# A one-core hybrid block: the gathered tile of the second layer is routed on its own, ahead of the three dense tiles

## The chip, the cores and the metric

The kernel runs as one program on one core of a Trainium2 chip. The metric is device time in microseconds (us) of one execution. The kernel before was timed three times: 4815.14, 4817.73 and 4818.47 us, median 4817.73 us.

Five engines have instruction streams of their own, each executed in order: PE (TensorE, matmuls; its weight loads are listed as PEld), DVE (VectorE), ACT (ScalarE), POOL (GpSimd) and SP (SyncE, which only issues DMAs here). They meet through semaphores.

## The reference

Two layers on 512 latent tokens (four tiles of 128) and 256 context tokens. Layer 0 mixes tokens with a gated delta rule, layer 1 with windowed attention. Each layer ends with a channel mixer that retrieves experts (PEER), cut here to its core:

```python
def peer_ffn(h, w_query, sub_keys, expert_u, expert_v):
    q = (t @ w_query).reshape(t_count, PEER_HEADS, 2, PEER_HALF)   # 8 heads, two halves of 128
    s = jnp.einsum('thpd,hpkd->thpk', q, sub_keys)                 # 128 keys for each half
    s1, i1 = lax.top_k(s[:, :, 0], 16)
    s2, i2 = lax.top_k(s[:, :, 1], 16)
    cand_s = s1[..., :, None] + s2[..., None, :]                   # 16 x 16 pairs
    top_s, pos = lax.top_k(cand_s, 16)                             # 16 experts for each head
    idx, gate = ..., softmax(top_s)                                # 128 experts for each token
    act = gelu(einsum('pkd,pd->pk', expert_u[idx], h)) * gate
    return einsum('pk,pkd->pd', act, expert_v[idx])
```

In layer 1 it runs for the four latent tiles; a last RMSNorm gives the output.

## The kernel before

**Two ways through the experts.** `peer` (L1327) treats the four tiles in two ways. Three of them are dense tiles: `dense` (L1245) multiplies them by all 16384 experts, 128 blocks of 128, and the chosen experts' gates lie in a mostly empty array G that `gates_dram` (L1204) builds and writes to DRAM. The fourth is the gathered tile: `gather_u` (L1139) and `gather_v` (L1175) fetch, for each of 128 slots, one row of `expert_u` (then of `expert_v`) for each token, with an indirect DMA that POOL issues (L1162, L1189). DVE multiplies a fetched u row tile by the token (`u`, L1164) and sums; PE multiplies v rows by the weights (`po`, L1196; 32 steps of 8 matmuls). Rows land in a ring of UV = 6 buffers.

**The stages of the mixer in layer 1**, as they follow each other:

1. Norm: `peer_norm` (L905) for each tile: mean square on ACT, scaling `xs` on DVE, transposes `pk` on PE, `hk`, and the split of the result into a high and a low half (`hi`, `lo`), so that three fp32r matmuls give one product of nearly full precision (`mm3`, L81).
2. Routing: `peer_route` (L942) goes through 16 queries (8 heads, two halves). For each one it loads 512 KB of weights, splits them (`wh` on ACT, L286; `wl`, L287, on DVE here), does 24 matmuls `pq` over all tiles at once, then scores `pss` for each tile, and for each tile DVE finds the top 16 of 128 with five instructions (L992 to L996, called a set below). After queries 7 and 15, `pairs_of` (L1052) picks 16 pairs for four heads of one tile (a call below: 54 instructions, nearly all on DVE). For the gathered tile the pairs are picked later, inside `gather_u`.
3. Gates: `gates_dram` for each dense tile, one-hot rows on DVE, POOL and ACT, and one matmul `pg` for each token (fp32, which the trace lists as two rows).
4. Dense: for each block of experts `up` does 24 matmuls `pu` (384 columns); for each half of eight blocks `pv` does 144 matmuls (512 columns). Up to 17 results of `up` may wait (RUN = 17), so the scheduler puts 20 `up` blocks (480 matmuls) ahead of the last gate matmul.
5. `finish` (L1115) adds the mixer's output to each tile, and `final` (L1308) norms the four tiles, which it reads back from DRAM.

**What sets the order.** A scheduler orders each engine's stream when the program is built. The gather is a generator: `tick` (L149) lets it go on by some steps at each `up` (from block 16 on) and each `pv` weight load, 1.1 steps each in layer 1. A step is one row fetched. `tick` takes the kinds in turn that `mix` names; for gates, mix "V" asks for v rows alone. Instructions of the gather are pinned to program order. In `peer` of before:

```python
cand = self.peer_route(l, dtiles + gtiles, h + [hk], hdram, p, "left", ps, "u", 3, tg, RAW, c1, nd)
...
for t, (xd, r, gate) in enumerate(gtiles):
    works.extend(self.gather_tile(l, xd, hdram[nd + t], cand[nd + t], gate, gp, rps))
```

So all four tiles share one routing pass, and the gather exists only from the dense stage on.

Of the kernel before, what the change touches and what calls it, by code (L numbers as in the profile page):

```python
# [8 lines left out]
F32 = mybir.dt.float32  # L9
# [9 lines left out]
D = 1024  # L19
# [16 lines left out]
ND = (3, 3)  # L36
UV = 6
EARLY = 6
NORM = 6
ADAF = 7  # L40
RUN = 17
PLAIN = {"out": (0, 1), "route": {"c": 1, "a": 0, "b": 0}}
HG = 4
# [4 lines left out]
CUT = 20  # L48
LATE = (9, 9)
POB = 1  # L50
# [5 lines left out]
LO = 16  # L56
TICK = {"norm": 0, "proj": 0, "z": (0, 0), "mat": (0, 0), "inv": (4, 4), "scan": (2, 4), "out": 2, "swa": 6, "route": 0, "gates": 1,
        ("u", 0): 1.6, ("v", 0): 1.6, ("u", 1): 1.1, ("v", 1): 1.1}

# [7 lines left out]
class Kern:  # L67
    def __init__(self, tc, A, out, dbg=None):
        self.tc, self.nc, self.A, self.out, self.dbg = tc, tc.nc, A, out, dbg or {}
        self.queue = self.nc.sync  # L70
        self.back = []
        self.turn = self.due = 0

    def dma(self, out, in_):
# [867 lines left out]
    def peer_route(self, l, tiles, h, hdram, p, side, ps, pt, bufs, tg, raw, pools, early=6):  # L942
# [74 lines left out]
    def scratch_uv(self, p):  # L1017

        t = lambda shape, dt: p.tile([128] + list(shape), dt, name="pairw", tag="uv", bufs=UV)
        ge, pd, sm = t((8, TOPK, TOPK), BF), t((8, TOPK, TOPK), BF), t((D,), F32)  # L1020
# [118 lines left out]
    def gather_u(self, l, hd, sel, p, ps, this):  # L1139
# [20 lines left out]
        for s in range(SLOTS):  # L1160
            u = p.tile([128, D], F32, name="u", tag="uv", bufs=UV)
            nc.gpsimd.indirect_dma_start(out=u, out_offset=None, in_=A["p_u"],  # L1162
# [12 lines left out]
    def gather_v(self, xd, gate, p, ps, made, j0, j1):  # L1175
# [4 lines left out]
        for j in range(j0, j1):  # L1180
# [5 lines left out]
            for g in range(4):  # L1186
                v = p.tile([128, D], F32, name="v", tag="uv", bufs=UV)
                t = 32 * g + j
# [9 lines left out]
            yield 1  # L1198
        acc = p.tile([128, D], F32, name="gacc", tag="uv", bufs=UV)
        for hf in range(2):  # L1200
            pin(nc.scalar.copy(acc[:, hf * 512:(hf + 1) * 512], po[hf]))
        self.finish(xd, acc, gate, p, UV, nc.gpsimd)

    def gates_dram(self, G, t, ids, gt, p, ps):  # L1204

# [39 lines left out]
    def dense(self, l, tiles, h, G, p, q, gp, ps, works):  # L1245
# [80 lines left out]

    def peer(self, l, gtiles, dtiles, gp, rps, tg):  # L1327

        nd, ng = len(dtiles), len(gtiles)
        with ExitStack() as ctx:  # L1330
            p = ctx.enter_context(self.pool("pp" + tg))
            ps = ctx.enter_context(self.pool("pps" + tg, space=PSUM))
            h = [p.tile([128, KT, 512], F32R, name=n) for n in ("hi", "lo")]
            hdram = [None] * nd + [self.dp.tile([128, D], F32, name=f"h{tg}{t}") for t in range(ng)]
            G = self.dp.tile([32, 128, nd * 4, 4, 32], F32, name=f"G{l}")
            with ExitStack() as c1:
                with ExitStack() as c2:
                    hk = None
                    if PLAIN["route"][tg]:
                        hk = c2.enter_context(self.pool("ph" + tg, "right")).tile([128, KT, 128 * (nd + ng)], F32, name="hk")  # L1340
                    cand = self.peer_route(l, dtiles + gtiles, h + [hk], hdram, p, "left", ps, "u", 3, tg, RAW, c1, nd)
                q = c1.enter_context(self.pool("pb" + tg))
                for t in range(nd):
                    if t == LATE[l]:
                        cand[nd:] = [self.pairs(*c) for c in cand[nd:]]
                    self.gates_dram(G, t, *cand[t], q, ps)
                if LATE[l] == nd:
                    cand[nd:] = [self.pairs(*c) for c in cand[nd:]]
            with ExitStack() as c1:
                q = c1.enter_context(self.pool("pd" + tg))  # L1350
                works = []
                for t, (xd, r, gate) in enumerate(gtiles):
                    works.extend(self.gather_tile(l, xd, hdram[nd + t], cand[nd + t], gate, gp, rps))
                at = len(self.back) - (l == 0 and CUT > 0 and len(self.back) > 1)
                self.back[at:at] = works
# [189 lines left out]
```

## Time and profile before

| | |
|---|---|
| median of three runs | 4817.73 us |
| profiled execution, its time | 4825.25 us |
| its span (first to last instruction) | 4823.5 us |
| granted TensorE clock, mean | 0.935 |
| PE busy | 4180.6 us (87%) |
| DVE busy | 3134.1 us (65%) |
| ACT busy | 1966.9 us (41%) |
| POOL busy | 1559.0 us (32%) |

The busy time is the union of an engine's instructions. A PE that is busy all the time is not yet a PE at its best rate, since ends of matmuls are modelled and overlap; how far apart consecutive matmuls start says more. Layer 1's mixer takes the last third of the span, from 3311 us on.

### The profile page before, as it was taken

The page shows a single profiled execution, that of the slowest core. Times are in us where ns is not written, and L with a number is a line of the kernel's source. Part 1 is how long each engine was busy: PE and PEld are TensorE (multiplying, and loading weights), DVE is VectorE, ACT ScalarE, POOL GpSimd, SP SyncE. Part 2 cuts the span into 40 slices and gives each one's busy share as a digit, 9 for nine tenths or more (in the row PEclk, how much of TensorE's full clock was granted, in tenths as well). Part 3 has the DMA queues.
Part 4 walks back from the last instruction along what each step waited for, and adds up shares of the span by engine and source line. Part 5 has one row for each costly group of instructions (what it writes and reads, how often), then busy time and mean ns, then how long its engine had stood idle before and what let it go on. Part 6 is the DMA issues. An engine that isn't in the chain of part 4 may idle for free. (4 is left out here: it accounts for less than half of the span.)

```text
span 4823.5 us, 66222 instructions
## 1 busy us (share of the span) xinstructions
PE 4180.6 (87%) x23628; PEld 3439.8 (71%) x23628; DVE 3134.1 (65%) x7357; ACT 1966.9 (41%) x3632; POOL 1559.0 (32%) x1393
## 2 busy tenths in 40 slices
PE   7989998457787779999999947797987999999997
PEld 5867777346566569888887725565875898988886
DVE  4664569975798688666764324565986987744444
ACT  5755553322326843333332212443378433333332
POOL 0000022753466652444543332000155343222221
PEclk9989999778899989999999978898999999999999
DMA  6725644978876797899988876102245898766775
GB/s 245 232 94 188 227 143 148 328 261 309 310 267 231 228 339 256 330 340 336 354 318 311 289 248 206 62 18 78 89 127 141 289 346 296 282 243 251 248 260 208
DMA packets 412922, 1142.76 MB, mean 237 GB/s; under 512 B 36656, under 2 KB 152240, under 8 KB 412592
## 3 DMA queue, kind: packets, MB, share of 16 engines
q1 hardware_dynamic: 254352, 563.84, 33.6%
q0 software_dynamic: 158240, 574.69, 33.1%
q8 instruction: 186, 3.05, 0.3%
q14 instruction: 144, 1.18, 0.1%
HBM read 1050.83 MB, written 87.56 MB: 236 GB/s over the span
## 5 line engine op out<-in xcount | busy, mean ns | idle before, releaser
L286 ACT CAST wh<-w 128x1024 fp32r<-128x1024 f32 x636 | 663.7, 1048 | 1248.9 <-PE pu L84 567.6
L287 DVE TENSOR_TENSOR wl<-w,wh 128x1024 fp32r<-128x1024 f32 x604 | 736.0, 1223 | 508.9 <-ACT wh L286 493.1
L1162 POOL DMA_INDIRECT u<-p_u,idx x512 | 641.8, 1254 | 780.7 <-DVE u L1164 418.2
L1189 POOL DMA_INDIRECT v<-p_v,idxT x512 | 532.3, 1040 | 1005.8 <-PE po L1196 681.5
L83 PE MATMUL pu<-lo,wh 128*128 128x384 f32 x2048 | 698.0, 341 | 52.2 <-ACT a L1263 42.4
L1164 DVE SCALAR_TENSOR_TENSOR u<-u,hg 128x1024 f32<-128x1024 f32 x512 | 621.2, 1224 | 185.9 <-DMA u<-p_u,idx 181.5
L85 PE MATMUL pu<-hi,wl 128*128 128x384 f32 x2048 | 697.1, 341 | 10.0 <-POOL wl L287 8.2
L84 PE MATMUL pu<-hi,wh 128*128 128x384 f32 x2048 | 694.6, 339 | 0.0
L83 PE MATMUL pv<-wl,ah 128*128 128x512 f32 x1536 | 600.8, 393 | 2.7 <-DVE acc L1302 2.7
L84 PE MATMUL pv<-wh,ah 128*128 128x512 f32 x1536 | 602.6, 392 | 0.0
L85 PE MATMUL pv<-wh,al 128*128 128x512 f32 x1536 | 602.4, 392 | 0.0
L83 PEld LDWEIGHTS pu<-lo,wh 128*128 128x128 f32 x2048 | 390.0, 190 | 82.1 <-ACT a L1263 54.5
L85 PEld LDWEIGHTS pu<-hi,wl 128*128 128x128 f32 x2048 | 390.0, 190 | 36.7 <-issue 14.9
L84 PEld LDWEIGHTS pu<-hi,wh 128*128 128x128 f32 x2048 | 390.0, 190 | 9.7 <-issue 3.4
L83 PEld LDWEIGHTS pv<-wl,ah 128*128 128x128 f32 x1536 | 289.0, 188 | 81.0 <-issue 12.6
L1196 PE MATMUL po<-v,W 128*32 128x512 f32 x2048 | 267.9, 642 | 90.8 <-DMA v<-p_v,idxT 89.4
L85 PEld LDWEIGHTS pv<-wh,al 128*128 128x128 f32 x1536 | 288.8, 188 | 66.4 <-issue 7.5
L84 PEld LDWEIGHTS pv<-wh,ah 128*128 128x128 f32 x1536 | 288.9, 188 | 58.3 <-issue 4.2
L1239 PE MATMUL pg<-oa,ob 128*128 128x128 f32 x1536 | 267.1, 313 | 72.5 <-POOL ob L1235 47.7
L1239 PEld LDWEIGHTS pg<-oa,ob 128*128 128x128 f32 x1536 | 215.8, 203 | 129.7 <-POOL ob L1235 70.1
L95 ACT CAST ah<-a 128x384 fp32r<-128x384 f32 x256 | 130.9, 514 | 434.2 <-PE pv L84 395.3
L1238 ACT ACTIVATE ob<-hot,gT 128x128 f32<-128x128 bf16 x576 | 253.0, 529 | 18.2 <-DVE hot L1227 15.7
(488 smaller groups left out, 7405.3 us busy)
## 6 DMA issues: line engine op xcount, KB each, us to landing
w<-p_ut SPq DMA_DIRECT2D x256, 512.0 KB, 5.3
w<-p_vt SPq DMA_DIRECT2D x256, 512.0 KB, 5.1
w<-adaw SPq DMA_DIRECT2D x96, 512.0 KB, 5.4
G<-st SPq DMA_DIRECT2D x24, 2048.0 KB, 9.1
Gt<-G SPq DMA_DIRECT2D x64, 768.0 KB, 7.0
w<-g_qkv SPq DMA_DIRECT2D x48, 512.0 KB, 4.8
w<-p_wq SPq DMA_DIRECT2D x32, 512.0 KB, 4.8
w<-g_z SPq DMA_DIRECT2D x16, 512.0 KB, 4.1
```

What stands on the lines that cost most here:

```text
L83: mm(out, lh, rl, start=start, stop=False)
L84: mm(out, lh, rh, start=False, stop=False)
L85: mm(out, ll, rh, start=False, stop=stop)
L95: self.nc.scalar.copy(hi, x)
L286: nc.scalar.copy(hi, w)
L287: (sub or nc.vector).tensor_sub(lo, w, hi)
L1162: nc.gpsimd.indirect_dma_start(out=u, out_offset=None, in_=A["p_u"], in_offset=bass.IndirectOffsetOnAxis(ap=idx[:, s:s + 1], axis=0))
L1164: pin(nc.vector.scalar_tensor_tensor(u, u, 1.0, h, op0=OP.mult, op1=OP.mult, accum_out=w[:, s:s + 1]))
L1189: nc.gpsimd.indirect_dma_start(out=v, out_offset=None, in_=A["p_v"], in_offset=bass.IndirectOffsetOnAxis(ap=idxT[:, t:t + 1], axis=0))
L1196: pin(nc.tensor.matmul(po[hf][32 * g:32 * g + 32, :], W[:, g, :], vs[g][:, hf * 512:(hf + 1) * 512], start=j == j0, stop=j == j1 - 1, tile ...
L1238: nc.scalar.mul(ob[:, j, :], hot[:, :, b % 2 * 4 + j], gT[:, c0 + j:c0 + j + 1])
L1239: nc.tensor.matmul(pg[:, j, :], ob[:, j, :], oa[:, j, :], start=True, stop=True)
```

## The change

The second layer's `peer` is called with `first=True`. Then the gathered tile is normed and routed by a pass of its own (tag "bf", 128 columns, its own weight loads and splits, its pairs picked in the pass), its gather is put into the list of works at once, and the three dense tiles are routed after that, with `tick` letting two rows go on at each query. The first layer's call keeps its order.

```diff
-UV = 6
+RING = (6, 7)
-LATE = (9, 9)
-TICK = {... "route": 0, "gates": 1,
-        ("u", 0): 1.6, ("v", 0): 1.6, ("u", 1): 1.1, ("v", 1): 1.1}
+TICK = {... "route": {"c": 0, "a": 0, "bf": 0, "b": 2}, "gates": (1, 2),
+        ("u", 0): 1.6, ("v", 0): 1.6, ("u", 1): 0.9, ("v", 1): 0.9}
...
-            self.tick(TICK["route"], MIX["route"])
+            self.tick(TICK["route"][tg], MIX["route"])
...
-                    self.tick(TICK["gates"], MIX["gates"])
+                    self.tick(TICK["gates"][l], MIX["gates"])
...
-    def peer(self, l, gtiles, dtiles, gp, rps, tg):
+    def peer(self, l, gtiles, dtiles, gp, rps, tg, first=False):
...
-            h = [p.tile([128, KT, 512], F32R, name=n) for n in ("hi", "lo")]
+            T = 128 * (nd if first else nd + ng)
+            h = [p.tile([128, KT, T], F32R, name=n) for n in ("hi", "lo")]
...
+            if first:
+                with ExitStack() as c1:
+                    q = c1.enter_context(self.pool("pf" + tg))
+                    f = [q.tile([128, KT, 128 * ng], F32R, name=n) for n in ("fhi", "flo")]
+                    cand = self.peer_route(l, gtiles, f + [None], hg, p, "left", ps, "u", 3, tg + "f", RAW, c1, ng)
+                gathered(cand)
+                self.back.extend(works)
             with ExitStack() as c1:
+                tiles, hd = (dtiles, [None] * nd) if first else (dtiles + gtiles, [None] * nd + hg)
...
-                    cand = self.peer_route(l, dtiles + gtiles, h + [hk], hdram, p, "left", ps, "u", 3, tg, RAW, c1, nd)
+                    cand = self.peer_route(l, tiles, h + [hk], hd, p, "left", ps, "u", 3, tg, RAW, c1, nd)
...
-                self.peer(1, tl[:4 - ND[1]], tl[4 - ND[1]:], gp, rps, "b")
+                self.ring = RING[1]
+                self.ip = c1.enter_context(self.pool("ids1"))
+                self.peer(1, tl[:4 - ND[1]], tl[4 - ND[1]:], gp, rps, "b", True)
```

The streams of all engines are the same up to the norm of layer 1's mixer. Three places show what moves.

DVE, from the last instructions of attention's output (`x<-x,y`, L748) on; `nss` and `xs` are the norm, `wl` a weight split, `top` and `ti` the top 16. Before:

```order
L748 TENSOR_TENSOR x<-x,y 128x256
L914 RECIPROCAL nss<-nss 128x1
L915 TENSOR_SCALAR xs<-xs,nss 128x1024
L914 RECIPROCAL nss<-nss 128x1
L915 TENSOR_SCALAR xs<-xs,nss 128x1024
L287 TENSOR_TENSOR wl<-w,wh 128x1024
L926 TENSOR_SCALAR hk<-pk,col_77 128x128
L287 TENSOR_TENSOR wl<-w,wh 128x1024
```

DVE at the same place after the change:

```order
L748 TENSOR_TENSOR x<-x,y 128x256
L914 RECIPROCAL nss<-nss 128x1
L915 TENSOR_SCALAR xs<-xs,nss 128x1024
L287 TENSOR_TENSOR wl<-w,wh 128x1024 x2
L926 TENSOR_SCALAR hk<-pk,col_77 128x128 x4
L932 TENSOR_TENSOR flo<-hk,fhi 128x1024
L287 TENSOR_TENSOR wl<-w,wh 128x1024 x2
L992 MAX top_27926<-sc 128x8
L993 MAX_INDEX ti_27927<-top_27926,sc 128x8
```

The pass of the one tile stands where the norm of the four stood, behind the last instruction of attention; so it does on PE and on ACT. The norm of the dense tiles now stands behind the whole pass, its pairs included.

POOL, from the load of the gathered tile's tokens (`hg`, L1148) to the tile's end; `ob` belongs to the gates, `u` and `v` are the fetched rows. Before:

```order
L1148 DMA hg<-hb_27863 128x1024
L287 TENSOR_TENSOR wl<-w,wh 128x1024 x16
L1235 TENSOR_SCALAR ob<-hot,gT 128x128 x96
L1162 DMA u<-p_u,idx 128x1024 x128
L1189 DMA v<-p_v,idxT 128x1024 x128
```

POOL after the change:

```order
L1148 DMA hg<-hb_27866 128x1024
L1162 DMA u<-p_u,idx 128x1024 x39
L287 TENSOR_TENSOR wl<-w,wh 128x1024 x16
L1235 TENSOR_SCALAR ob<-hot,gT 128x128 x96
L1162 DMA u<-p_u,idx 128x1024 x89
L1189 DMA v<-p_v,idxT 128x1024 x128
```

39 of the 128 u fetches moved ahead of the first dense weight splits and the gates; none stands among the gates. On DVE 32 of the 128 products `u` stand ahead of the gates, 4 in the norm of the dense tiles and 28 in their routing, two in each query.

SP, the last DMAs: `x_105` is the gathered tile in DRAM, `x_106` to `x_108` the dense tiles; `x<-` is a load of `final`, `out<-y` a store of it. Before:

```order
L75 DMA x<-x_105 128x1024
L75 DMA w<-p_vt 128x1024
L75 DMA out<-y 128x1024
L1124 DMA x_106<-xf 128x1024
L1124 DMA x_107<-xf 128x1024
L75 DMA x<-x_106 128x1024
L1124 DMA x_108<-xf 128x1024
L75 DMA x<-x_107 128x1024
L75 DMA out<-y 128x1024
L75 DMA x<-x_108 128x1024
```

SP after the change:

```order
L1124 DMA x_106<-xf 128x1024
L1124 DMA x_107<-xf 128x1024
L1124 DMA x_108<-xf 128x1024
L75 DMA x<-x_105 128x1024
L75 DMA x<-x_106 128x1024
L75 DMA out<-y 128x1024
L75 DMA x<-x_107 128x1024
L75 DMA out<-y 128x1024
L75 DMA x<-x_108 128x1024
```

The gathered tile's load in `final` moved from ahead of the last dense weights to behind the last stores of the dense tiles, and the other loads stand behind it. On PE the last two of the gather's 32 steps (16 matmuls `po`) stand behind the last `pv`; before, the last step stood 162 `pv` ahead of it.

## Rows read from the trace of the kernel before

**Rows 1.** Windows, layer 1's mixer by stage: length, busy (instructions), clock, DMA, GB/s
```profile
core 0: us, PE busy (x) PEld busy (x) DVE busy (x) ACT busy (x) POOL busy (x), PEclk, DMA share, GB/s
3311.00:3342.00 31.00, 10.60 (x41) 7.80 (x41) 15.85 (x30) 19.76 (x37) 0.00 (x0) 0.52 0.48 170
3342.00:3451.00 109.00, 108.34 (x534) 92.10 (x535) 93.13 (x535) 33.16 (x50) 5.32 (x3) 0.98 0.28 93
3451.00:3541.00 90.00, 73.75 (x359) 70.43 (x359) 89.55 (x371) 35.46 (x56) 39.01 (x16) 0.87 0.27 88
3541.00:3728.00 187.00, 158.14 (x880) 125.80 (x878) 142.72 (x207) 176.77 (x359) 106.21 (x94) 0.97 0.49 141
3728.00:3744.00 16.00, 0.00 (x0) 0.00 (x0) 3.22 (x7) 2.63 (x5) 0.00 (x0) 0.52 0.87 280
3744.00:4798.00 1054.00, 1049.75 (x5410) 898.48 (x5410) 641.38 (x966) 354.17 (x486) 296.80 (x259) 1.00 0.75 271
4798.00:4823.50 25.50, 0.00 (x0) 0.00 (x0) 11.40 (x13) 4.33 (x9) 0.00 (x0) 0.55 0.50 185
```

**Rows 2.** Timeline, PE in one query: start, us, engine, line, out<-in, shape, count
```profile
3367.69 1.06 PE L986 MATMUL pss<-sk,qT 128*128 128x128 f32 x8
...
3369.05 0.39 PE L85 MATMUL pq<-hi,wl 128*128 128x512 f32 x1
...
3374.04 1.06 PE L986 MATMUL pss<-sk,qT 128*128 128x128 f32 x8
```

**Rows 3.** Timeline, PE, dense: a run of 46 matmuls of 384 columns
```profile
3842.36 0.33 PE L85 MATMUL pu<-hi,wl 128*128 128x384 f32 x1
...
3850.36 0.39 PE L83 MATMUL pv<-wl,ah 128*128 128x512 f32 x1
```

**Rows 4.** Timeline, PE: attention's projection, matmuls of 256 columns
```profile
2961.47 0.28 PE L85 MATMUL pj<-wh,lo 128*128 128x256 f32 x1
2961.59 0.28 PE L83 MATMUL pj<-wl,hi 128*128 128x256 f32 x1
```

**Rows 5.** Groups of PE by line, dense stage: busy us, mean ns, idle before
```profile
L84 PE MATMUL pv<-wh,ah 128*128 128x512 f32 x768 | 301.3, 392 | 0.0
L84 PE MATMUL pu<-hi,wh 128*128 128x384 f32 x864 | 290.8, 337 | 0.0
L1196 PE MATMUL po<-v,W 128*32 128x512 f32 x512 | 62.6, 598 | 0.0
```

**Rows 6.** Timeline around attention's end and the norm of the four tiles
```profile
3310.54 0.32 SPq L75 DMA_DIRECT2D x<-x  x1
...
3319.06 0.75 DVE L915 TENSOR_SCALAR xs<-xs,nss 128x1024 f32<-128x1024 f32 x1
...
3327.76 1.22 DVE L932 TENSOR_TENSOR lo<-hk,hi 128x1024 fp32r<-128x1024 f32 x1 [0.52 <-ACT hi L931]
...
3340.67 1.22 DVE L932 TENSOR_TENSOR lo<-hk,hi 128x1024 fp32r<-128x1024 f32 x1 [1.11 <-ACT hi L931]
```

**Rows 7.** Timeline, DVE: first and last rows of one query's four sets
```profile
3357.17 0.87 DVE L992 MAX8 top<-sc 128x8 f32<-128x128 f32 x4
...
3361.65 0.29 DVE L996 FIND_INDEX8 ti<-top,wk 128x8 uint32<-128x128 f32 x1
```

**Rows 8.** Groups of DVE by line, 3342 to 3541 us: the weight splits
```profile
L287 DVE TENSOR_TENSOR wl<-w,wh 128x1024 fp32r<-128x1024 f32 x14 | 17.1, 1221 | 16.0 <-ACT wh L286 16.0
```

**Rows 9.** Tile u: ns min/median/max, first to last start
```profile
L1162 POOL DMA_INDIRECT u<-p_u,idx x128: 934/1088/1988, 3800.8 to 4185.7; - x128
L1164 DVE SCALAR_TENSOR_TENSOR u<-u,hg x128: 1210/1218/1261, 3807.9 to 4211.0; 128x1024 f32<-128x1024 f32 x128
```

**Rows 10.** DMA issues from 3600 us on: KB, median us to landing
```profile
u<-p_u,idx POOLq DMA_INDIRECT x128, 7.3
v<-p_v,idxT POOLq DMA_INDIRECT x128, 6.1
...
x<-x SPq DMA_DIRECT2D x4, 512.0 KB, 4.6
```

**Rows 11.** Timeline, the tail: POOL's store, DVE's last sum and last output
```profile
4768.89 0.54 POOL L1124 DMA_DIRECT2D x<-xf  x1 [7.48 <-DVE xf L1123]
...
4798.69 0.69 DVE L1302 TENSOR_TENSOR acc<-pv,acc 128x512 f32<-128x512 f32 x1
...
4818.20 1.29 DVE L1324 SCALAR_TENSOR_TENSOR y<-x,ss,fg 128x1024 f32<-128x1024 f32 x1
```

More of the change, by code (lines that the diff above doesn't have):

```diff
@@ L41 @@
 RUN = 17
-PLAIN = {"out": (0, 1), "route": {"c": 1, "a": 0, "b": 0}}
+PLAIN = {"out": (0, 1), "route": {"c": 1, "a": 0, "b": 0, "bf": 0}}
 HG = 4
@@ L56 @@
 LO = 16
-TICK = {"norm": 0, "proj": 0, "z": (0, 0), "mat": (0, 0), "inv": (4, 4), "scan": (2, 4), "out": 2, "swa": 6, "route": 0, "gates": 1,
-        ("u", 0): 1.6, ("v", 0): 1.6, ("u", 1): 1.1, ("v", 1): 1.1}
+TICK = {"norm": 0, "proj": 0, "z": (0, 0), "mat": (0, 0), "inv": (4, 4), "scan": (2, 4), "out": 2, "swa": 6, "route": {"c": 0, "a": 0, "bf": 0, "b": 2}, "gates": (1, 2),
+        ("u", 0): 1.6, ("v", 0): 1.6, ("u", 1): 0.9, ("v", 1): 0.9}
 MIX = {"proj": "uv", "z": ("uv", "uv"), "norm": "uv", "mat": ("uv", "uv"), "inv": ("uv", "uv"), "scan": ("uv", "uv"), "out": "v", "swa": "v", "route": "v", "gates": "V", "dense": "uv"}
@@ L72, in __init__ @@
         self.turn = self.due = 0
+        self.ring = RING[0]
     def dma(self, out, in_):
@@ L1017, in scratch_uv @@
     def scratch_uv(self, p):
-        t = lambda shape, dt: p.tile([128] + list(shape), dt, name="pairw", tag="uv", bufs=UV)
+        t = lambda shape, dt: p.tile([128] + list(shape), dt, name="pairw", tag="uv", bufs=self.ring)
         ge, pd, sm = t((8, TOPK, TOPK), BF), t((8, TOPK, TOPK), BF), t((D,), F32)
@@ L1160, in gather_u @@
         for s in range(SLOTS):
-            u = p.tile([128, D], F32, name="u", tag="uv", bufs=UV)
+            u = p.tile([128, D], F32, name="u", tag="uv", bufs=self.ring)
             nc.gpsimd.indirect_dma_start(out=u, out_offset=None, in_=A["p_u"],
@@ L1186, in gather_v @@
             for g in range(4):
-                v = p.tile([128, D], F32, name="v", tag="uv", bufs=UV)
+                v = p.tile([128, D], F32, name="v", tag="uv", bufs=self.ring)
                 t = 32 * g + j
@@ L1198, in gather_v, with gates_dram @@
             yield 1
-        acc = p.tile([128, D], F32, name="gacc", tag="uv", bufs=UV)
+        acc = p.tile([128, D], F32, name="gacc", tag="uv", bufs=self.ring)
         for hf in range(2):
             pin(nc.scalar.copy(acc[:, hf * 512:(hf + 1) * 512], po[hf]))
-        self.finish(xd, acc, gate, p, UV, nc.gpsimd)
-    def gates_dram(self, G, t, ids, gt, p, ps):
+        self.finish(xd, acc, gate, p, self.ring, nc.gpsimd)
+    def gates_dram(self, l, G, t, ids, gt, p, ps):
         nc = self.nc
@@ L1304, in dense @@
         for t in range(nd):
-            self.finish(tiles[t][0], acc[t], tiles[t][2], gp, UV, nc.sync)
+            self.finish(tiles[t][0], acc[t], tiles[t][2], gp, self.ring, nc.sync)
     def final(self, X):
@@ L1332, in peer, with gathered @@
             ps = ctx.enter_context(self.pool("pps" + tg, space=PSUM))
-            h = [p.tile([128, KT, 512], F32R, name=n) for n in ("hi", "lo")]
-            hdram = [None] * nd + [self.dp.tile([128, D], F32, name=f"h{tg}{t}") for t in range(ng)]
+            T = 128 * (nd if first else nd + ng)
+            h = [p.tile([128, KT, T], F32R, name=n) for n in ("hi", "lo")]
+            hg = [self.dp.tile([128, D], F32, name=f"h{tg}{t}") for t in range(ng)]
             G = self.dp.tile([32, 128, nd * 4, 4, 32], F32, name=f"G{l}")
+            works = []
+            def gathered(cand):
+                for t, (xd, r, gate) in enumerate(gtiles):
+                    works.extend(self.gather_tile(l, xd, hg[t], cand[t], gate, gp, rps))
+            if first:
[5 more added lines that the diff above has]
+                self.back.extend(works)
             with ExitStack() as c1:
+                tiles, hd = (dtiles, [None] * nd) if first else (dtiles + gtiles, [None] * nd + hg)
                 with ExitStack() as c2:
@@ L1339, in peer @@
                     if PLAIN["route"][tg]:
-                        hk = c2.enter_context(self.pool("ph" + tg, "right")).tile([128, KT, 128 * (nd + ng)], F32, name="hk")
-                    cand = self.peer_route(l, dtiles + gtiles, h + [hk], hdram, p, "left", ps, "u", 3, tg, RAW, c1, nd)
+                        hk = c2.enter_context(self.pool("ph" + tg, "right")).tile([128, KT, T], F32, name="hk")
+                    cand = self.peer_route(l, tiles, h + [hk], hd, p, "left", ps, "u", 3, tg, RAW, c1, nd)
                 q = c1.enter_context(self.pool("pb" + tg))
                 for t in range(nd):
[L1344 to L1348, printed above, removed]
+                    self.gates_dram(l, G, t, *cand[t], q, ps)
             with ExitStack() as c1:
                 q = c1.enter_context(self.pool("pd" + tg))
[L1351 to L1355, printed above, removed]
+                if not first:
+                    gathered(cand[nd:])
+                    at = len(self.back) - (l == 0 and CUT > 0 and len(self.back) > 1)
+                    self.back[at:at] = works
                 self.dense(l, dtiles, h, G, p, q, gp, ps, works)
```

## The prediction, made before the changed kernel ran

> **What bounds the kernel now.** I read the windows of layer 1's mixer first, one for each stage, then the starts of consecutive matmuls, then DVE's groups and timeline, then the gather's tiles and DMAs, and last the tail. Everything ahead of 3311 us keeps its order, so only these 1512 us count.
>
> The dense stage, 3744 to 4798 us, belongs to PE: 1049.75 of 1054 us busy at full clock, while DVE works 641, ACT 354 and POOL 297 us [rows 1]. Busy time alone proves little, so take the starts. From 3369.05 to 3374.04 us PE starts 22 matmuls of 512 columns, 0.227 us each [rows 2]; 46 of 384 columns take 8.00 us, 0.174 each [rows 3]; 256 columns take 0.12 [rows 4]. That is 0.42 ns for a column, the 2.4 GHz level, and some 13 ns for each matmul. With three groups of 864 `pu`, three of 768 `pv` and the `po` [rows 5]: 2592 x 0.174 + 2304 x 0.227 + 62.6 = 1037 us. All stalls together have 17 us. Nothing in the dense stage waits for the gather.
>
> Ahead of it stand four stretches [rows 1]. The norm (31 us) is a chain of short steps. The 109 us of queries are PE's at first: a query takes 3374.04 - 3367.69 = 6.35 us [rows 2], of which DVE's four sets take (3361.65 + 0.29 - 3357.17) = 4.77 us [rows 7]. The 90 us after that are DVE's (89.55 busy), with pairs. The gates' 187 us are ACT's (176.77 busy). So what is late from 3342 to 3541 us is DVE with 93.13 + 89.55 = 182.7 us of work and 16.0 us of waiting for split weights [rows 1, 8].
>
> **The change, part by part.**
>
> *The pass of the one tile is new and serial.* PE, ACT and DVE execute it behind attention's last instructions, as the rows of the order show; behind the store at 3310.54 us [rows 6] nothing else is left to run beside it. From the first scaling, 3319.06 us, to the end of the first tile's `lo`, 3327.76 + 1.22, are 9.9 us; to the end of the fourth's, 22.8 us [rows 6]. So its first `pq` comes near 3329 us.
>
> Its DVE work: 16 splits of 1.22 us [rows 8], 16 sets of 4.77 / 4 = 1.19 us [rows 7], and two calls of `pairs_of`. Price of a call: 182.7 us less 64 sets (76.2) and 14 splits (17.1) leaves 89 us for 271 of the 326 pair instructions that the order counts for three tiles, 0.33 us each, 54 in a call: 17.5 us. Sum 16 x 2.41 + 35 = 74 us, the lower end.
>
> What PE needs for a 128-column fp32r `pq` no row shows. From below, the line through the 256 and 512 columns gives 0.067 us; the nearest rows say 0.12 (256 columns) and, from above, 0.20 to 0.22: an fp32 `pss` of 128 columns is listed as two rows, eight of which take 0.8 to 0.9 us [rows 2, 4]. I take 0.12, the nearest in kind. A query then has 24 x 0.12 + 0.2 = 3.1 us on PE against 2.41 on DVE, and with the hand-over of two split buffers (a cast, a split, then matmuls) 3.3 us. The first eight queries take 26 us; in the last eight DVE has a call of pairs as well, 2.41 + 17.5 / 8 = 4.6 us, 37 us; 4 us fill the pipeline, and 46 of the second call's 54 instructions stand behind the last set, 15 us. In all 82 us.
>
> *The norm of the three dense tiles* comes after that, since DVE's stream has it behind the pairs: 9.9 + 2 x 4.3 = 18.5 us by [rows 6], and four products `u` of 1.22 us stand in it, half of them in gaps: 21 us. The dense pass starts its first `pq` at 3329 + 82 + 21 = 3432 us where it was 3342: +90 us.
>
> *The routing of the dense tiles* loses a quarter of its sets and gains rows. DVE: 14 splits 17.1, 48 sets 57.1, 262 pair instructions with the gates' first steps 86.4, 28 products `u` of 1.22 us [rows 9] 34.2, together 195 us against 182.7. PE has 24 x 0.174 + 0.4 = 4.6 us in a query against DVE's 1.22 + 3.57 + 2.44 = 7.2, so DVE no longer waits for it; of the 16 us of waits I leave 5, for rows that land 7.3 us after their issue [rows 10] and for the fill. 200 us against 199: +1 us. Its bounds: no wait at all (-4), or 15 us more, since POOL's 16 splits of dense weights now stand behind 39 fetches, the last of which wait for buffers, and two scores stand behind the `pu` that need these splits.
>
> *The gates* fetch nothing: their `tick` asks for v rows alone, and v rows need all 128 u rows. ACT's work is the same. 0 us.
>
> *The dense stage* has the same 2592 `pu` and 2304 `pv`. 96 products, not 128, and no pairs of the gathered tile are left in it; these lie on DVE (641 of 1054 us busy [rows 1]), beside PE's work. They can give back at most the 17 us of stalls; I take 3. Two of the 32 `po` steps, 62.6 / 32 = 2 us each [rows 5], leave it for the tail: 4. Together -7 us.
>
> *The tail* is where the slower pace of 0.9 rows shows. It was 25.5 us [rows 1]; the gathered tile had been stored at 4768.89 us, long ahead [rows 11]. Now, counted from the last `pv`: the last sums and a weight tile (2 us), one `po` step (2), then the last fetch, whose buffer that step frees (1.1 to issue [rows 9], 6.1 to land [rows 10]), the last step on a PE back at half clock (0.55 in the tail [rows 1]) (3), two copies and two products (3.6), the store (4), and at 22 us the load, with the three other loads behind it in SP's queue. Before, from the first of these loads to the end were 19 us; a fourth tile in the two buffers adds some 2. About 43.5 us: +18, between +10 and +24.
>
> Sum: 90 + 1 - 7 + 18 = +102 us on the profiled execution's 4825.25 us, 4927 us. That execution lay 7.5 us above the median of the three runs, so the forecast is **4920 us**, 2.1% slower.
>
> **A rule of the skill against this sum.** By the trace the dense stage is at PE's rate, because its starts are as far apart as the columns take. The Trainium skill (Perfetto Trace Analysis, Identifying the Most-Contended Engine) says that busy matmul time does not tell how near PE is to its limit, and that its headroom is to be judged by the share of weight loads, among others. That share is 898.48 of 1054 us here, and read so 15% would be free. What this would make of the time is the third rival.
>
> **The rivals.**
>
> First: narrow fp32r matmuls run like fp32, at 0.20 to 0.22 us. For it: the `pss` rows. Against: from 512 down to 256 columns the time falls in step with the columns. A query takes 24 x 0.21 + 0.2 = 5.2 us on PE, the pass 16 x 5.2 + 19 = 102 to 109 us, 20 to 27 more: 4943 us.
>
> Second: DVE waits for rows in routing. Its stream is in order, so a late row holds the sets behind it, and with them the scores and `pq`. For it: a row lands 7.3 us after its issue, and 128 rows took 410 us in the dense stage, 3.2 us each [rows 9, 10]. Against: that was the pace that `tick` asked for, and a ring of seven lets POOL run two to three queries ahead. At 2 us for each of 14 pairs: 28 us more, 4948 us.
>
> Third, on the other side: PE in the dense stage is not at its limit; it is slowed by casts and splits that the gather's DVE work delays. With 32 products and the pairs gone it would fall towards the 898 us of its weight loads, 156 us less [rows 1], and the change would end at 4920 - 156 = 4764 us. It decides from 102 us returned on. For it: DMA share and DVE are highest early in that stage. Against: the starts, which leave 17 us in all.
>
> Fourth: the one tile's pass costs nothing because its steps fill gaps beside attention's last block. Then 82 + 10 us fall away, 4828 us. The order on PE, ACT and DVE stands against it.
>
> **How the numbers follow.** Forecast 0.65, first rival 0.22, second 0.08, third 0.03, fourth 0.02. The lower end takes the pass at 74 us (-8), no wait in routing (-5), half of the stalls given back (-5) and a tail of +10 (-8): 4894, and some more below for the shorter waits of the norm: 4885. The upper end is the first two rivals with a longer tail: 4955. A change of 0.2%, some 10 us, is what a measurement of this kernel can tell. Faster is the third rival, 0.03; within 0.2% is what the fourth would give with a little more returned (its 4828 us lie just outside), 0.02; slower 0.95.
>
> **What the profile after would show.** Right: the first 128-column `pq` near 3329 us, the first `pq` of 384 columns near 3432, the first gate matmul some 90 us after 3541 and the gates again 187 us long; some 32 products `u` ahead of them and none among them; `pu` and `pv` starts unchanged at 0.174 and 0.227; a tail of over 40 us that begins with two `po` steps. The spacing of the new `pq` decides between the forecast and the first rival; DVE's waits for `u` in routing show the second. The forecast is wrong if the dense stage is shorter by 30 us or more, or if the new pass starts ahead of 3311 us.

## The result and the profile after

The changed kernel takes 4965.77 us (median of four runs, 4963.38 to 4968.06); before, measured beside it, takes 4818.1 us. The ratio is 1.030, 95% interval 1.0285 to 1.0314: slower, as forecast, but 46 us above the 4920 us and outside the range of 4885 to 4955 us. Its profiled execution took 4967.13 us, with a span of 4965.4 us.

Below are the windows of the changed kernel, by stage as in [rows 1]: the one tile's pass in halves, its trailing pairs, the norm of the dense tiles, their routing in halves, gates, dense, tail.

```profile
core 0: us, PE busy (x) PEld busy (x) DVE busy (x) ACT busy (x) POOL busy (x), PEclk, DMA share, GB/s
...
3331.60:3375.00 43.40, 43.40 (x204) 43.40 (x204) 17.44 (x55) 9.47 (x20) 0.53 (x1) 0.50 0.36 122
3375.00:3419.40 44.40, 44.40 (x210) 44.40 (x209) 32.06 (x138) 12.86 (x27) 0.00 (x0) 0.50 0.32 107
3419.40:3438.00 18.60, 1.68 (x6) 1.08 (x5) 16.74 (x86) 6.15 (x13) 0.00 (x0) 0.50 0.23 85
3438.00:3465.80 27.80, 5.68 (x26) 4.67 (x26) 15.44 (x31) 9.54 (x18) 12.87 (x11) 0.56 0.60 210
3465.80:3570.00 104.20, 84.42 (x466) 81.22 (x467) 96.50 (x410) 28.25 (x45) 43.28 (x29) 0.92 0.68 228
3570.00:3671.00 101.00, 83.19 (x421) 79.46 (x420) 100.05 (x418) 42.09 (x64) 40.45 (x17) 0.90 0.25 88
3671.00:3858.00 187.00, 155.36 (x853) 122.49 (x852) 143.29 (x212) 174.81 (x356) 98.68 (x94) 0.96 0.49 138
...
3876.00:4917.00 1041.00, 1040.52 (x5375) 895.05 (x5373) 580.41 (x796) 345.70 (x474) 234.00 (x216) 1.00 0.69 248
4917.00:4965.40 48.40, 5.57 (x32) 1.09 (x32) 15.79 (x19) 8.12 (x15) 2.66 (x4) 0.57 0.63 229
```

The first two lines are the surprise. In the new pass PE is busy for all of 87.8 us, DVE for 49.5, and the granted clock is 0.50, the 1.2 GHz level, from end to end. PE's timeline in the pass, to be set against [rows 2 to 4]:

```profile
3331.87 0.41 PE L84 MATMUL pq<-fhi,wh 128*128 128x128 f32 x1
3332.08 0.41 PE L85 MATMUL pq<-fhi,wl 128*128 128x128 f32 x1
3332.29 0.41 PE L83 MATMUL pq<-flo,wh 128*128 128x128 f32 x1
```

One `pq` starts 0.213 us behind another, 384 times, so a query takes 5.55 us, where 3.3 were forecast for the first eight. This is not one execution's chance: in e4, e6 and e10 below, whose pass has the same instructions, it takes 87.7 us from first to last `pq` again, at 0.50. The waits in the same stretch (us in total, times, longest) show the chain:

```profile
ACT wh L286 <- PE pq L84: 53.6, 14, 5.5
DVE wl L287 <- ACT wh L286: 35.6, 12, 6.3
```

DVE waits 35.6 us in this pass alone for `wh` (16.0 in the whole routing before [rows 8]), and ACT to write `wh`, for PE to be done with its buffer. PE is the bound here, not DVE.

To compare executions I count from the first scaling of the mixer (`xs`, 3319.06 us before [rows 6]), since this point itself lies between 3315.7 and 3328.2 us in executions whose order up to there is the same. In us, from first starts of each stage; in "forecast" the prediction's terms are put into the same form:

| | before | forecast | after |
|---|---|---|---|
| `xs` to the pass's first `pq` | | 9.9 | 7.1 |
| first `pq` to last pair | | 82 | 105.6 |
| from there (before: from `xs`) to the dense tiles' first `pq` | 22.9 | 21 | 28.5 |
| routing, to the first `pg` | 199.8 | 200.8 | 205.6 |
| gates and dense, to the last `pv` | 1255.5 | 1248.5 | 1244.8 |
| tail | 26.3 | 44.3 | 49.2 |
| total | 1504.4 | 1606.5 | 1640.9 |

So 34 us are missed inside the mixer, 24 of them in the pass. The rest of the 46 us is where the executions lie: the mixer begins 5.4 us later in the profiled execution of after, and the profiled one of before was 7.5 us above its median, that of after 1.4 above its own.

The norm of the dense tiles, as a timeline (in brackets idle time and its releaser), has a wait that [rows 6] did not have:

```profile
3438.28 1.57 POOL L1162 DMA_INDIRECT u<-p_u,idx  x1 [102.46 <-DVE nss L914]
...
3448.96 1.22 DVE L1164 SCALAR_TENSOR_TENSOR u<-u,hg 128x1024 f32<-128x1024 f32 x1 [6.27 <-DMA u<-p_u,idx]
...
3465.76 0.69 PE L83 MATMUL pq<-lo,wh 128*128 128x384 f32 x1 [6.27 <-DVE lo L932]
```

The first fetched row is used 10.7 us after its issue starts (the median to landing was 7.3 [rows 10]). DVE, in order, waits 6.27 us for it, and the rest of the norm stands behind.

The tail, as a timeline, beside [rows 11]:

```profile
4917.50 1.92 PE L1196 MATMUL po<-v,W 128*32 128x512 f32 x16 [0.98 <-DVE W L1182]
...
4919.68 0.95 POOL L1189 DMA_INDIRECT v<-p_v,idxT  x1 [6.51 <-PE po L1196]
...
4924.48 3.64 PE L1196 MATMUL po<-v,W 128*32 128x512 f32 x16 [5.05 <-DMA v<-p_v,idxT]
...
4941.48 1.25 SPq L75 DMA_DIRECT2D x<-x  x2
...
4960.11 1.28 DVE L1324 SCALAR_TENSOR_TENSOR y<-x,ss,fg 128x1024 f32<-128x1024 f32 x1
```

It is the chain that was forecast: a step, the last fetch, a step, the sums, the stores, then the loads. The fetches themselves, as the tile's view lists them (beside [rows 9]; ns min/median/max, first to last start):

```profile
L1162 POOL DMA_INDIRECT u<-p_u,idx x128: 943/1022/3014, 3438.3 to 4254.7; - x128
L1164 DVE SCALAR_TENSOR_TENSOR u<-u,hg x128: 1200/1218/1232, 3449.0 to 4288.7; 128x1024 f32<-128x1024 f32 x128
```

The gather starts 363 us sooner than before and ends 78 us later on DVE.

### The profile page after: what moved, and what is told of

Read it like the earlier page. It is cut to its first block, busy times and chain, and to the rows that moved or that the text cites. A ratio compares the mean times of both kernels' runs of the same rounds, so it can differ in the third digit from the quotient of the medians.

```text
span 4965.4 us, 67193 instructions
## 1 busy us (share of the span) xinstructions
PE 4251.2 (86%) x24012; PEld 3518.2 (71%) x24012; DVE 3165.3 (64%) x7407; ACT 1991.6 (40%) x3684; POOL 1555.6 (31%) x1393
## 5 line engine op out<-in xcount | busy, mean ns | idle before, releaser
L286 ACT CAST wh<-w 128x1024 fp32r<-128x1024 f32 x652 | 680.2, 1048 | 1320.4 <-PE pu L84 561.0
L287 DVE TENSOR_TENSOR wl<-w,wh 128x1024 fp32r<-128x1024 f32 x620 | 756.5, 1223 | 591.6 <-ACT wh L286 549.8
```

The source lines that it names most:

```text
L286: nc.scalar.copy(hi, w)
L287: (sub or nc.vector).tensor_sub(lo, w, hi)
```

## Experiments

The diffs are shortened: `...` and plain names stand for what is left out. Windows have the columns of the table of windows above where nothing else is said.

Two theories for the pass. A: the 128-column `pq` is dear because of the granted clock. B: a narrow fp32r matmul costs 0.21 us at either level, as the prediction's first rival had it.

**e1: wider matmuls between.**

```diff
                 self.mm(pq, ...)
+                if tg == "bf":
+                    for _ in range(2):
+                        nc.tensor.matmul(bank[:, 128:512], self.identb, iotae[:, 0:384], start=True, stop=True)
```

> The changed kernel with two more matmuls (384 columns, bf16) behind each of the eight steps of a query in the one-tile pass; they write the unused part of the same PSUM bank, and nothing reads it. Question: why are the 128-column pq 0.215 us apart, where 0.12 was forecast? Theory A: the granted clock, 0.50 in the whole pass; at the 2.4 GHz level a 128-column pq takes 0.107 to 0.12 us. If the wider matmuls bring the clock up, the three pq of a step then start 0.107 to 0.12 us apart and a query takes 24 x 0.11 + 16 x 0.17 = 5.4 us, no longer than now although it has 16 matmuls more. Theory B: a narrow fp32r matmul costs 0.215 us at either level: then the clock reads 1.0, the three pq of a step stay 0.215 us apart, and a query takes 24 x 0.215 + 16 x 0.17 = 7.9 us. If the clock stays at 0.50 all the same, a query takes about 24 x 0.215 + 16 x 0.33 = 10.4 us and the run tells the two apart only by the edges of the pass.

The added matmuls share a PSUM bank with `pq` and change the results of this run; which sums they change was not traced, so it is used for starts and clock alone. Windows of the pass, and PE late in it:

```profile
3323.30:3328.00 4.70, 4.69 (x20) 4.02 (x21) 0.00 (x0) 0.00 (x0) 0.53 (x1) 0.50 0.44 143
3328.00:3408.30 80.30, 80.30 (x648) 72.53 (x646) 49.13 (x193) 22.34 (x47) 0.00 (x0) 1.00 0.37 117
```
```profile
3380.22 0.27 PE L84 MATMUL pq<-fhi,wh 128*128 128x128 f32 x1
3380.33 0.28 PE L85 MATMUL pq<-fhi,wl 128*128 128x128 f32 x1
3380.44 0.50 PE L975 MATMUL pq<-iotae,identb 128*128 128x384 bf16 x2
```

From 3328 us on the clock is 1.00, and `pq` starts 0.11 us apart, so B is refuted. The pass, with 256 matmuls more, takes 85.0 us from first to last `pq`, against 87.7. The one execution took 4957.61 us.

**e5: the same without a price.** Sixteen wide matmuls once, ahead of the first `pq`.

```diff
+            if tg == "bf" and m == 0:
+                for _ in range(16):
+                    nc.tensor.matmul(pq, self.identb, iotae[:, 0:512], start=True, stop=True)
```

> The changed kernel with sixteen matmuls of 512 columns (bf16) on PE behind the norm of the gathered tile and ahead of the first pq; the first pq overwrites what they write, so all results stay. They take 16 x 0.43 = 6.9 us at the 1.2 GHz level and start some 3 to 5 us ahead of where pq starts now. Question: the changed kernel's stream of 128-column pq stayed at a granted clock of 0.50; in the run with wider matmuls between, the clock rose to 1.00 and pq fell to 0.11 us apart. If the stream only cannot raise the clock but keeps one that was raised: pq 0.11 us apart in the whole pass, a query 3.0 us on PE, the pass some 80 us instead of 106, and the time 20 to 25 us under the changed kernel, 4941 to 4946 us. If the stream of 128-column matmuls lets a raised clock fall again: pq goes back to 0.213 us within the first queries, the pass ends 2 to 5 us later than in the changed kernel, and the time is 4966 to 4971 us.

4928.48 us, ratio to before 1.0219 (1.0203 to 1.0235). Windows: the wide matmuls, the first query, the rest of the pass:

```profile
3323.80:3327.90 4.10, 4.07 (x13) 1.65 (x13) 1.11 (x1) 0.83 (x2) 0.00 (x0) 0.67 0.63 228
3327.90:3334.00 6.10, 6.10 (x55) 5.90 (x53) 1.23 (x1) 1.43 (x3) 0.53 (x1) 1.00 0.27 86
3334.00:3375.30 41.30, 40.98 (x365) 40.58 (x363) 39.01 (x165) 20.93 (x45) 0.00 (x0) 1.00 0.61 196
```

The stream of 128-column matmuls did not raise the clock in the changed kernel, but here it kept a raised one (e10 lost it). The pass falls from 105.6 to 70.9 us up to its last pair. The mixer takes 33.2 us less than in the changed kernel, and the medians (of runs on different occasions) differ by 37 us; 20 to 25 were expected. A is shown: behind the sixteen added matmuls the pass has the same instructions, at the other clock.

**e2: 256 columns for the same result.** The tile stands twice side by side, and half of the product is not read.

```diff
+            nc.scalar.copy(hi[:, :, 128:256], hi[:, :, 0:128])
+            nc.vector.tensor_copy(lo[:, :, 128:256], lo[:, :, 0:128])
...
-            pq = ...[:, 0:T]
+            pq = ...[:, 0:256]
```

> The changed kernel, but the one-tile pass multiplies 256 columns: the tile stands twice side by side, and the second half of the product is not read. Twice the columns for the same result. Theory A (the clock): if the wider matmuls bring the clock up, a pq takes 0.12 us as the 256-column ones elsewhere, a query 24 x 0.12 + 0.3 = 3.2 us on PE, DVE's 2.4 to 4.6 us become the bound, and the pass falls from 106 to about 82 us: 20 to 25 us less than the changed kernel, some 4943 us. If the clock stays at 0.50, a 256-column pq takes 0.22 to 0.24 us and the pass stays at 106 to 112 us: 0 to +6 us. Theory B (a floor of 0.215 us for each fp32r matmul under 256 columns, whatever the clock): the same 0.12 us if the clock is up; e1 tells it from A.

4930.29 us, 1.0213 (1.0194 to 1.0232). PE's first `pq` and some later ones:

```profile
3333.48 0.41 PE L84 MATMUL pq<-fhi,wh 128*128 128x256 f32 x1
3333.70 0.41 PE L85 MATMUL pq<-fhi,wl 128*128 128x256 f32 x1
...
3350.01 0.28 PE L84 MATMUL pq<-fhi,wh 128*128 128x256 f32 x1
3350.13 0.28 PE L85 MATMUL pq<-fhi,wl 128*128 128x256 f32 x1
```

Twice the columns in less time: 50.5 us from first to last `pq` instead of 87.7. The kernel takes 35 us less than the changed one, where 20 to 25 were expected. At a clock of 0.50 a `pq` of 256 columns starts 0.213 us behind another, exactly as one of 128; at 1.00 0.120 against 0.111. So 128 columns cost as much as 256 at 0.50, and only 0.009 us less at 1.00.

**e10: what sets that floor?** 192 matmuls of several widths ahead of the pass, overwritten by it; one execution, 4989.86 us.

```diff
+                for n, a, b in ((16, identb, io[:, 0:512]), (32, identb, io[:, 0:256]), (32, identb, io[:, 0:128]),
+                                (32, identb, io[:, 0:64]), (16, identb, io[:, 0:512]),
+                                (32, wh[:, 0, :], hi[:, 0, 0:64]), (32, wh[:, 0, :], hi[:, 0, 0:128])):
+                    for _ in range(n):
+                        nc.tensor.matmul(pq[:, 0:width], a, b, start=True, stop=True)
```

> The changed kernel with 192 matmuls ahead of the one-tile pass's first pq, overwritten by it: 16 of 512 columns (bf16), then 32 each of 256, 128 and 64 columns (bf16, one weight tile), 16 of 512 again, then 32 each of 64 and 128 columns in fp32r. Question: a 128-column pq took as long as a 256-column one, 0.213 us at a granted clock of 0.50 and 0.111 against 0.119 at 1.00. If that is the time of a weight load in fp32r, the bf16 matmuls of 128 and 64 columns fall with the columns, to 0.06 and 0.03 us at a clock of 1.00, and the fp32r ones of 64 columns stay at 0.11. If any matmul has a floor of 0.11 us (its issue), bf16 shows it too. If narrow fp32r is slower for each column, 64 columns take half of 128's time.

Windows over these matmuls alone (length, PE, PEld, clock, DMA share, GB/s), in bf16 512, 256, 128 and 64 columns, then fp32r 64 columns:

```profile
3325.90:3328.46 2.56, 2.56 (x6) 0.91 (x6) 0.50 0.64 251
3330.64:3334.13 3.49, 3.49 (x33) 3.12 (x32) 1.00 0.45 150
3334.13:3335.91 1.78, 1.78 (x34) 1.78 (x32) 1.00 0.00 0
3335.92:3336.84 0.92, 0.92 (x35) 0.92 (x33) 1.00 0.00 0
...
3340.22:3343.79 3.57, 3.57 (x34) 3.54 (x33) 1.00 0.00 0
```

Each stretch holds the starts of 32 (the first of 6). In bf16 the time falls with the columns, 0.109, 0.056 and 0.029 us; in fp32r 64 columns take 0.112 us like 128. So it is neither a floor of every matmul nor a price for each column; a floor by each fp32r matmul's weight load fits (in bf16, too, a load is listed for each matmul, but the starts are as close as 0.029 us). The Trainium skill (TensorE: Matmul & The Clock Gate, LDWEIGHTS) has a load take its columns divided by 1.2 GHz, by which 128 columns take an estimated 107 ns, and says under Weight-path perf modes that the fast weight load is on only for types other than fp32. The traces are near this at a clock of 1.00 (0.111 us); at 0.50 the floor is 0.213, which that figure does not give. No run changed the weight load alone, so that the load is the cause stays argued.

In the same run the clock fell back to 0.50 near 3345.5 us, behind 32 `pq`-like matmuls of 64 columns and 16 of 128, without an idle moment on PE, and stayed there for the pass:

```profile
3343.80:3345.40 1.60, 1.60 (x17) 1.60 (x16) 0.00 (x0) 0.00 (x0) 0.00 (x0) 1.00 0.00 0
3345.60:3350.00 4.40, 4.40 (x23) 4.40 (x22) 0.00 (x0) 0.00 (x0) 0.00 (x0) 0.50 0.00 0
```

Why e5 kept its clock through 384 matmuls of 128 columns and this run lost it, these runs don't settle.

**e3: plain fp32 in the pass.** 8 `pq` in a query, each listed as two rows, and no `wh` or `wl`.

```diff
-PLAIN = {... "route": {"c": 1, "a": 0, "b": 0, "bf": 0}}
+PLAIN = {... "route": {"c": 1, "a": 0, "b": 0, "bf": 1}}
```

> The changed kernel, but the one-tile pass multiplies in fp32 without the split into halves: 8 matmuls pq in a query instead of 24, and no wh on ACT and no wl on DVE. If the pass is bound by PE's rate of 24 narrow matmuls (both A and B), it becomes bound by DVE: 16 sets of 1.2 us and two calls of pairs, 16 x 1.2 + 2 x 17.5 = 54 us, or by the weight loads of 512 KB; with the fill 62 to 80 us instead of 106: 25 to 40 us less than the changed kernel, 4926 to 4940 us. If what bounds it is the chain of hand-overs for a query (load, cast, split, matmuls, copy, scores, set) rather than the number of matmuls, less than 15 us.

4912.71 us, 1.0179 (1.0162 to 1.0196), below the 4926 to 4940 us expected: the changed kernel's mixer less 48.5 us. Windows of the pass, its second line with the clock up:

```profile
3328.20:3335.60 7.40, 5.33 (x36) 5.17 (x35) 0.00 (x0) 1.12 (x4) 0.53 (x1) 0.80 0.56 171
3335.60:3368.30 32.70, 29.85 (x252) 28.56 (x251) 25.43 (x158) 9.37 (x31) 0.00 (x0) 1.00 0.79 256
```

The pass takes 40.0 us to its last `pq` and 63.0 to its last pair, at the lower end of what was expected, 42.6 us less than in the changed kernel. The other 6 us are a first `pq` 1.9 us earlier (no split ahead of it) and norm and routing 4.2 us shorter behind it.

**e4: the pace.**

```diff
-        ("u", 0): 1.6, ("v", 0): 1.6, ("u", 1): 0.9, ("v", 1): 0.9}
+        ("u", 0): 1.6, ("v", 0): 1.6, ("u", 1): 1.1, ("v", 1): 1.1}
```

> The changed kernel with the gather's pace in the dense stage back at 1.1 steps for each up and weight load, as before the change; all else as changed. My theory: the tail of 48.4 us instead of 25.5 is due to the pace of 0.9 alone, which left two of the 32 po steps behind the last pv. Then the tail is back at 25 to 28 us, the gathered tile's store lies ahead of the last pv, and the time falls by 18 to 23 us, to 4943 to 4948 us; the dense stage grows by at most 4 us (the two po steps). Rival: the faster pace brings more products and fetches beside PE's matmuls and gives the gain back there: less than 10 us.

4950.45 us, 1.0268 (1.0248 to 1.0287). The tail is 26.5 us, 22.8 less, as expected; but from the first `pg` to the last `pv` it takes 1258.6 us instead of 1244.8. Between starts, `po` takes 5.7 us more up to the last `pv` (two more steps), `pu` 5.8 and `pv` 2.6 us (stalls). Expected were 4 us; the rival holds for more than half: counted from `xs` the pace brings 9.0 us. The stalls do not belong to the pace alone: e6 and e9 below have this pace and the same number of instructions on PE, DVE, ACT and POOL from the first `pg` to the last `pv`, yet take 1262.1 and 1254.1 us there. These runs don't show why, so a few us in that stage settle nothing.

**e6: no rows in routing**, with the pace of 1.1 as in e4.

```diff
-"route": {"c": 0, "a": 0, "bf": 0, "b": 2}
+"route": {"c": 0, "a": 0, "bf": 0, "b": 0}
```

> The run with the pace of 1.1, and no row is asked for in the routing of the dense tiles: the gather fetches from the dense stage on, as before the change. All else as changed. Compared with that run from the norm of the dense tiles to the first gate matmul. My theory: 28 products u of 1.22 us (34 us of DVE) and the wait of 6.3 us in the norm go with the rows; the routing is then bound as before by DVE with 17 + 57 + 86 = 160 us and PE's 16 x 4.6 us, some 165 to 180 us instead of 205, so the first gate matmul comes 30 us earlier. In the dense stage 32 products and fetches come back beside PE: +3 to +6 us. In all 20 to 30 us less than the run with the pace of 1.1: 4920 to 4930 us. Rival: the rows fill gaps in which DVE waits for split weights anyway (16 us of waits before): then the first gate matmul comes at most 15 us earlier and the time is 4935 us or more.

4913.81 us, 1.0187 (1.0171 to 1.0202). Windows of norm and routing:

```profile
3431.40:3446.90 15.50, 5.60 (x25) 4.59 (x25) 10.62 (x22) 9.21 (x18) 0.00 (x0) 0.61 0.10 34
3446.90:3621.90 175.00, 155.97 (x864) 151.92 (x865) 162.71 (x768) 67.81 (x106) 43.57 (x18) 0.94 0.29 97
```

Against e4 the norm is 13.1 us shorter and the routing 30.3; up to the last `pv` 3.5 us come back. In all 39.9 us from norm to last `pv`, more than the 20 to 30 expected. So the rows that were fetched early cost 43 us in front, where DVE is late. Behind, where PE is late, they save 3.5 us by this pair of runs, less than the 8 us between e6 and e9, so it is not shown that they save anything there.

**e7: the dense tiles' norm ahead of the one-tile pass**, plain fp32 as in e3.

```diff
-            for t, (xt, row, _) in enumerate(tiles):
+            for t, (xt, row, _) in enumerate([] if tg == "b" else tiles):
...
+                for t, (xt, row, _) in enumerate(dtiles):
+                    s = slice(t * 128, (t + 1) * 128)
+                    self.peer_norm(l, xt, row, h[0][:, :, s], h[1][:, :, s], None, None, n, ps, "u", 3)
                 ...
                 cand = self.peer_route(l, gtiles, ...)
```

> The run with the plain fp32 pass, and the norm of the three dense tiles stands ahead of the one-tile pass instead of behind its pairs. Behind the pass the first pq of 384 columns then needs split weights alone. My theory: the 26 to 28 us between the last pair and that first pq are a serial chain of the second norm; put ahead, the norm of three tiles takes 13 to 14 us there (4.3 a tile), and the first pq comes 2 to 5 us behind the pairs, or even beside them: 8 to 12 us less than the plain run, 4900 to 4905 us. Rival: the three norms are late in either place, and the wait for u rows moves into the routing: within 4 us of the plain run.

4921.47 us, 1.0195 (1.0179 to 1.0211); counted from `xs` 1591.9 us against 1592.4. The first dense `pq` came 49.8 us behind the pass's last one in e3 (23.0 of pairs, 26.8 of norm) and comes 3.7 us behind it here, but the pass starts 17 us later, and the routing takes 226.6 us instead of 203.1, with DVE full:

```profile
3395.10:3621.70 226.60, 171.88 (x890) 163.59 (x890) 220.97 (x932) 70.44 (x112) 94.67 (x57) 0.90 0.50 172
```

The rival's size holds from `xs` (the medians, of runs on different occasions, lie 9 us apart the other way), and DVE is the cause: the last pair now starts 28.5 us behind the first dense `pq`, so most of the trailing pairs moved into the routing.

**e9: three edits together**: the diffs of e3, e4 and e6.

> Three of the single edits at once: the one-tile pass in plain fp32, no rows fetched in the routing of the dense tiles, and the pace of 1.1. What stays of the change is the gathered tile's own pass alone. Measured from the first scaling of the mixer, the changed kernel needed 1640.9 us to its end; plain fp32 took 48.5 off, the rows another 40.2, the pace 9.1. If these are independent: 1640.9 - 97.8 = 1543 us, some 4862 to 4870 us, still 40 us over before. Theory: the rest is the pass itself, which stands alone on DVE's chain (two calls of pairs 35 and 16 sets 19 us, with the fill 63 us from its first pq to its last pair), less the 25 us that a routing of three tiles takes less than one of four. Rival: the pass is not the price, the gather beside the dense stage is: then the dense stage, not the front, is longer than before by tens of us.

4862.68 us, 1.0068 (1.0049 to 1.0088); 1539.6 us from `xs`, 1543 expected. The edits add up to within 4 us, the stages less well: gates and dense took 8 us less than in e6. What is left of the change costs 35.2 us over before: `xs` to the dense tiles' first `pq` 85.8 against 22.9 (+62.9), routing 173.5 against 199.8 (-26.3), gates and dense 1254.1 (-1.4), tail 26.3 (0). The dense stage is no longer than before, so the rival falls.

**e8 and e11: versions that were to beat both.** The kernel before with `wl` of layer 1's routing on POOL (e8), or with the last eight queries in plain fp32 (e11).

```diff
-            w = self.wsplit(p, A["p_wq"][l, m], "u", [KT, 128], raw, 2, plain=plain)
+            w = self.wsplit(p, A["p_wq"][l, m], "u", [KT, 128], raw, 2, nc.gpsimd if tg == "b" else None, plain=plain)
```
```diff
+PLAIN = {... "b": 1}
...
+            plain = PLAIN["route"][tg] and (tg != "b" or m >= 8)
             w = self.wsplit(p, A["p_wq"][l, m], "u", [KT, 128], raw, 2, plain=plain)
```

> The kernel before, with the low halves wl of layer 1's query weights computed on POOL instead of DVE; a try at a version that beats both. In routing DVE has 182.7 us of work and 16.0 us of waits for 199 us; 14 splits of 1.22 us leave it. If POOL, idle there but for 44 us, does a split in about 2 us without delaying the scores: 10 to 17 us less than before, 4803 to 4812 us. If a split on POOL slows DVE's instructions beside it, or comes late for pq (PE's 6.35 us a query bound the first half anyway): within 5 us of before, or slower.

> The kernel before, with the last eight queries of layer 1's routing multiplied in plain fp32, unsplit; a second try at a version that beats both. There DVE sets the pace (89.55 of 90 us busy) and PE has room. It saves 8 wl of 1.22 us, 9.8 us, and part of the 16.0 us that DVE waits for wh; PE takes 8 matmuls of 512 columns in fp32 for a query, at four times the 0.227 us 7.3 us, against 5.4. If DVE's work is what counts: 8 to 18 us less than before, 4807 to 4818 us. If PE becomes the bound there (7.3 + 1.06 = 8.4 us a query, 8 queries 67 us, less than the 90) or the wait only moves: within 5 us of before.

e8: 4825.48 us, 1.0004 (0.9995 to 1.0014). e11: 4827.0 us, 1.0000 (0.9989 to 1.0011). Neither beats before. In e8 DVE's wait moved (groups of DVE in routing; the first line is of before):

```profile
L1087 DVE TENSOR_TENSOR pd<-pd 128x512 bf16<-128x512 bf16 (+2 forms) x42 | 25.0, 596 | 0.2
...
L1087 DVE TENSOR_TENSOR pd<-pd 128x512 bf16<-128x512 bf16 (+2 forms) x42 | 26.6, 633 | 0.2
...
L992 DVE MAX8 top<-sc 128x8 f32<-128x128 f32 x64 | 14.0, 276 | 26.0 <-ACT sc L988 26.0
```

It waits 26.0 us for scores in place of 16.0 for `wh`, and the pair products beside POOL's splits take 633 ns instead of 596. In e11 the first `pg` comes 14.4 us sooner, and from there to the last `pv` it takes 15.5 us longer: before that `pg` PE did 260 `pu` instead of 380, so 120 had to be done later.

## Why the prediction was wrong, by its steps

**The step that failed** is PE's price in the pass: "What PE needs for a 128-column fp32r `pq` no row shows ... I take 0.12, the nearest in kind." It was 0.213. The 0.12 came from rows at a granted clock of 1.00 ([rows 4]; the trace has 1.00 from 2961 to 2962 us), and I applied it to a stretch that begins behind a norm at 0.52 [rows 1], without asking whether the new stream would bring the clock up. Why a stream that the trace lists as 100% busy did not do so stays open. With the clock up a `pq` takes 0.111 us (e5), so the price was right for 2.4 GHz; and the pass takes 70.9 us there where 82 were forecast (its queries 47.0 instead of 67, the pairs behind them 23.9 instead of 15). That e5 from `xs` takes 1607.6 us, beside the 1606.5 forecast, is luck in part: 11 us too many in the pass cancel 8.5 too few in the norm and 6 in the tail.

**The first rival** had the number, 102 to 109 us for the pass against 105.6, by a wrong mechanism: narrow fp32r is not as slow as fp32 at the same clock (at 1.00 a `pq` of 128 columns takes 0.111 us in e5, and in e3 two rows 0.112 us apart). What stood against it was half wrong: "the time falls in step with the columns" holds down to 256 and not below (e2, e10).

**The norm**, 21 us forecast, took 28.5. The four products were counted, the first row's landing time was not: DVE stands 6.27 of the 7.5 us for it. That is the second rival's mechanism, in the norm instead of in routing.

**Routing**, 200.8 forecast and 205.6 measured, was right in kind: DVE has 196.96 of 205.60 us busy, 195 were summed. e6 shows its two sides, which the net of +1 us hid: three tiles alone take 25 us less than four, the rows 30 more. In e2, e3 and e5 it took 201 to 203 us; what makes the 3 to 5 us difference is open.

**Gates** took 187 us as before, right. **Dense**: -10.7 us together with the gates, forecast -7. PE's weight loads have 895.05 of 1041 us, a share of 0.86 (0.85 before [rows 1]), and `pu` and `pv` start 0.173 and 0.227 us apart in the median, as before. So the third rival is refuted: 32 products and all pairs left that stage, and no 156 us came back. It was built on the rule of the Trainium skill (Perfetto Trace Analysis, Identifying the Most-Contended Engine) to judge headroom by this share, among others; read as 15% free, the share misleads in this stage.

**The tail** was +23 us, forecast +18 within +10 to +24: the chain was right, and the first load came 25.4 us behind the last `pv` instead of 22. What the prediction did not see is that the pace that lengthens the tail takes more off the dense stage than the two `po` steps: 13.8 us by e4, of which the stalls, some 8 us, are not steady (e9).

**The fourth rival** is refuted: nothing lies beside the pass. By e9 the pass alone costs 35 us over before, even without its clock, row and pace terms. By the sums from `xs`, the changed kernel's +136.5 us are about 48 for the 24 narrow matmuls of a query and their splits (33 of which a raised clock gives back, e5), 40 for the early rows, 9 for the pace, and 35 to 39 for a serial pass as such; the terms come from e3 to e6 and e9.

## What to carry to other kernels

Before pricing a new stream of matmuls from rows at 1.00, look at the granted clock of the stretch that it will follow, and do not take it for granted that the stream itself will raise it: a PE listed as busy was not enough here, and sixteen wide matmuls ahead were worth 33 us. A separate pass over fewer tiles pays its fixed parts again (weight loads, splits, fill, trailing pairs), so first find the engine beside which these could be hidden. Work that is fetched early is only free if it lands on the engine that isn't late there.

## What the runs showed of the hardware

- A stream of 128-column fp32r matmuls with PE 100% busy stayed at a granted clock of 0.50 for 87.8 us. 256-column fp32r, 512-column bf16 and plain fp32 matmuls of 128 columns were followed by a clock of 1.00 (e2, e5, e3). The Trainium skill (TensorE: Matmul & The Clock Gate, What's actually happening) has the gate set by how busy PE has been recently; by the busy time that the trace lists, that does not hold here.
- Start to start, fp32r with a weight load listed for each matmul: 64 columns 0.112 us, 128 0.111, 256 0.120 at 1.00; 128 and 256 both 0.213 at 0.50. bf16 at 1.00: 64 columns 0.029, 128 0.056, 256 0.109, 512 0.216.
